# Hybrid decoder trunk on one core: the accumulating transfer of weight quarters one group earlier, and the hooks moved

## The chip, the cores and the metric

One core of one Trainium2 chip. The metric is the device time of one execution of the kernel in microseconds (us); a smaller number is better. Several executions are timed, and one more is recorded by the hardware profiler.

## The reference

Two layers on an activation of 512 tokens by 2048 features, all in float32. Each layer does one input projection, three parallel branches, and one output projection onto the residual stream:

```
h = _rmsnorm(x, norm_g)
proj = h @ w_in                      # 2048 x 7696
y_conv = B * conv3(C * h_conv) * silu(gate)          # 512 wide
y_sb   = stick_breaking(rms(q), rms(k), v) * silu(gate)   # 8 heads of 128, 128-query blocks
y_gla  = rms(gated linear attention(q, k, v, decay)) * silu(gate)   # 4 heads, chunks of 64
return x + concat(y_conv, y_sb, y_gla) @ w_out       # 2048 x 2048
```

## The kernel before

**Groups.** The columns of both weights are cut into groups of 256: 30 of `w_in` and 8 of `w_out` in a layer, taken in one fixed order in the list `specs`: the linear attention's groups and the first half of the convolution's, then v, g, q, k for each pair of heads (j = 0 to 3), the second half of the convolution, and the output groups gi = 0 to 7. Between the groups of one j and the next lies the attention of that pair of heads: query and key tiles are normalised (squares on ACT in L1318, scaling on DVE in L1332), cast (L1336 on ACT, L1337 on DVE), transposed by DMA from SP's queue (L1341) and multiplied into scores on TensorE (L1226).

**Precision by splits.** Float32 is kept by splitting each weight into an fp16 high part (ACT) and an fp16 rest (DVE). A normal group has one high and one rest for each half of its rows (L435, L442) and takes three matmul passes. The common scale of a group comes first: the sum of squares of both halves of its staged tile (`squares`: two ACT instructions, L366, 1.9 us each), a reduction over partitions on POOL (L380), and a few tiny steps on DVE (`wscale`, L383 to L398).

**Quick groups.** Some groups are multiplied by seven products instead of eight (`project_quick`): the 2 by 2 blocks b11, b12, b21, b22 of the group's weights are combined, and seven combinations are split (`split` in `wsums`: L485 on ACT, L486 on DVE, once each for parts 0 to 6, the last into `w7h` and `w7l`). They are g and k for each j and `conv h 1` in `w_in`, and gi = 3, 4, 6 in layer 0 and 3, 4, 5, 6 in layer 1 of `w_out`. In the input groups b12 + b11 is formed by a DMA that accumulates, L503 on POOL's queue (half a megabyte); in the output groups by DVE adds (L492 to L498). The products go into four accumulators: pa holds product 1, is copied to y12 by ACT (L778) and later copied to y11 (L785); pb, pd and pf follow.

**Order.** Loads (`fetch`, L355, two halves of 1 MB, issued from POOL) go two groups ahead into two staging buffers `st`. A quick group alters its staged tile in place and holds the buffer until its last split. Within a group, matmuls call `hook`, which pops functions from a list that `weights` fills: the first takes the squares of the next group, the second its scale and its splits. `order` ties an instruction behind the matmul of the hook. Each engine runs its own list in order, and POOL's list holds loads, reductions and the accumulating transfers together.

```
# weights(), before
if i + 2 < len(specs):
    with tc.high_priority():
        fetch(i + 2)
if i and i + 1 < len(specs):
    hooks.extend([lambda mm: squares(i + 1, mm), lambda mm: parts_of(i + 1, mm)])
```

Of the kernel before, what the change touches and what calls it, by code (L numbers as in the profile page):

```python
# [11 lines left out]
ALU = mybir.AluOpType  # L12
# [31 lines left out]
def hybrid_trunk(ctx, tc, x, norm_g, w_in, conv_w, conv_b, sb_qn_g, sb_kn_g,  # L44
# [145 lines left out]
    def order(a, b):  # L190
        tc.add_manual_dep(a.ins, b.ins.name, mybir.DependencyInfo(
            mybir.DependencyClass.NoSync, mybir.DependencyReason.DATA), reason="order")
# [254 lines left out]
    def squares(i, mm):  # L447

        with tc.high_priority():
            for h in range(2):  # L450
                a = wmax(i, h)
                if not h:
                    order(a, mm)
# [12 lines left out]
    def hook(mm):  # L466

        if hooks:
            hooks.pop(0)(mm)

    def wsums(i):

        sc = scales[i]
        b11, b12, b21, b22 = (whole[i][:, r::2, c * P:(c + 1) * P] for r in range(2) for c in range(2))
        parts = loaded[i][0]
        for _ in range(3):
            a = [wpool.tile([P, HK, GX], F16, tag=t, name=nm(t)).rearrange("p k c -> p (k c)") for t in ("wh", "wl")]
            parts.extend([p_[:, n * HK * P:(n + 1) * HK * P] for p_ in a] for n in range(2))
        parts.append([wk([P, HK * P], t, 1, dt=F16) for t in ("w7h", "w7l")])
        for n in range(7):  # L480
            parts[n] = [a.rearrange("p (k c) -> p k c", c=P) for a in parts[n]]

        def split(b, n):
            h_, l_ = parts[n]
            hi = S.activation(h_, b, AF.Copy, scale=sc)  # L485
            V.scalar_tensor_tensor(l_, b, sc, h_, ALU.mult, ALU.subtract)  # L486
            return hi


        if specs[i][1] is w_out:  # L490
            split(b11, 0)
            V.tensor_tensor(b11, b11, b12, ALU.add)  # L492
            split(b22, 3)
            V.tensor_tensor(b12, b12, b22, ALU.add)
            V.tensor_tensor(b22, b11, b22, ALU.add)
            split(b22, 1)
            split(b12, 2)
            V.tensor_tensor(b22, b22, b21, ALU.add)  # L498
            split(b21, 4)
            split(b11, 5)  # L500
            split(b22, 6)
            return
        G.dma_start(out=b12, in_=b11, accum_op=ALU.add)  # L503
        split(b11, 0)
        split(b22, 3)
        V.tensor_tensor(b22, b12, b22, ALU.add)  # L506
        split(b22, 1)
        V.tensor_tensor(b11, b22, b11, ALU.subtract)
        split(b11, 2)
        split(b21, 4)  # L510
        V.tensor_tensor(b21, b22, b21, ALU.add)
        split(b12, 5)
        split(b21, 6)

    def weights():

        i = cursor[0]
        cursor[0] += 1
# [3 lines that stand above are left out]
        assert not hooks  # L522
        if i and i + 1 < len(specs):
            hooks.extend([lambda mm: squares(i + 1, mm), lambda mm: parts_of(i + 1, mm)])
        return loaded.pop(i)

    fetch(0)
# [129 lines left out]
    for l in range(depth):  # L657
# [3 lines left out]
        def project_cols():  # L661

            w, u = weights()
            ps = [bank(psp, "p") for _ in range(2)]
            for h in range(2):
                wh, wl = w[h]
                for c, o in enumerate(ps):
                    cs = slice(c * P, (c + 1) * P)
                    for kk in range(HK):
                        k = h * HK + kk  # L670
                        st_ = (h == 0 and kk == 0)
                        en = (h == 1 and kk == HK - 1)
                        T.matmul(o, wh[:, kk, cs], xh[:, :, k, :], start=st_, stop=False)  # L673
                        T.matmul(o, wh[:, kk, cs], xl[:, :, k, :], start=False, stop=False)  # L674
                        mm = T.matmul(o, wl[:, kk, cs], xh[:, :, k, :], start=False, stop=en)  # L675
                        if not h and not c and kk in (0, HK - 1):
                            hook(mm)
            return ps, u

# [7 lines left out]
        def project_toks(ah, al, late=()):  # L687

            w, u = weights()
            ps = [bank(psp, "p") for _ in range(2)]  # L690
            rounds = [[k for k in range(h * HK, (h + 1) * HK) if k not in late] for h in range(2)] + [list(late)]
            lastk = [q for q in rounds if q][-1][-1]
            for ks in rounds:
                for t in range(NT):
                    o = ps[t // 2][:, (t % 2) * GW:(t % 2 + 1) * GW]
                    for k in ks:
                        mm = tok_mm(o, ah, al, w, t, k, GW, k == 0 and t % 2 == 0, k == lastk)
                        if not t and k == 0 or t == 1 and k == rounds[0][-1]:
                            hook(mm)
            return ps, u  # L700

# [47 lines left out]
        def project_quick(src, sums, y, cols):  # L749

            (w11, wT2, wT3, w22, w21, wt1, wT4), u = weights()
            (pa, pd), (pb, pf) = ([bk[:, n * GW:(n + 1) * GW] for n in range(2)]
                                  for bk in [bank(psp, "p") for _ in range(2)])
            a11, a12, a22 = ([a[:, 2 * r:2 * r + 2, c::2, :] for a in src] for r, c in ((0, 0), (0, 1), (1, 1)))
            s_, a21_22, a12_s, a11_21 = sums

            def prod(o, w, a, start, stop=False):
                for t in range(1 if cols else 2):
                    for kk in range(HK):
                        for i, (p_, q_) in enumerate(((0, 0), (0, 1), (1, 0))):  # L760
                            st_ = start and t == kk == i == 0
                            en = stop and kk == HK - 1 and i == 2
                            if cols:
                                mm = T.matmul(o, w[q_][:, kk, :], a[p_][:, :, kk, :], start=st_, stop=en,  # L764
                                              skip_group_check=True)
                            else:
                                mm = T.matmul(o[:, t * P:(t + 1) * P], a[p_][:, t, kk, :], w[q_][:, kk, :], start=st_,  # L767
                                              stop=en, skip_group_check=True)
                            if start and t == kk == 0 and i == 2 and o is pa:
                                hook(mm)  # L770
                return mm

            y11, y12, y21, y22 = (
                y[:, c, r * GW:(r + 1) * GW] if cols else y[:, 2 * r:2 * r + 2, c * P:(c + 1) * P]
                for r in range(2) for c in range(2))
            za, zb, zd, zf = (a if cols else a.rearrange("p (t c) -> p t c", c=P) for a in (pa, pb, pd, pf))
            prod(pa, w11, a11, True)
            S.activation(y12, za, AF.Copy)  # L778
            hook(prod(pb, wT2, s_, True))
            V.tensor_tensor(y21, zb, y12, ALU.subtract)  # L780
            prod(pd, wT3, a11_21, False)
            S.activation(y22, zd, AF.Copy)
            prod(pf, w22, a12_s, False)
            prod(pa, w21, a12, False)
            S.activation(y11, za, AF.Copy)  # L785
            prod(pb, wt1, a21_22, False, True)
            V.tensor_tensor(y12, zb, y12, ALU.subtract)
            V.tensor_tensor(y22, y12, y22, ALU.subtract)
            V.tensor_tensor(y12, zf, y12, ALU.add)
            yield 0, u  # L790
            prod(pd, wT4, a22, False, True)
            V.tensor_tensor(y21, zd, y21, ALU.subtract)
            yield 2, u
# [12 lines left out]
        def project_by_token(ah, al, n):  # L806

            w, u = weights()
            ps = []
            for t in range(NT):  # L810
                o = bank(psp, "p")
                for i, (a_, part) in enumerate(((ah, 0), (al, 0), (ah, 1))):
                    for k in range(KT):
                        mm = T.matmul(o[:, :n], a_[:, t, k, :], w[k // HK][part][:, k % HK, :n],  # L814
                                      start=i == 0 and k == 0, stop=i == 2 and k == KT - 1)
                        if not t and (not i and not k or i == 2 and k == KT - 1):
                            hook(mm)
                ps.append(o)
                yield t, o, u
# [611 lines left out]
```

## Time and profile before

| | |
|---|---|
| median of 3 runs | 1715.83 us (1713.79 to 1720.53) |
| the profiled execution | 1717.69 us |
| its span, first to last instruction | 1715.9 us |
| TensorE (PE) busy | 1669.9 us, 97% |
| VectorE (DVE) busy | 1331.3 us, 78% |
| ScalarE (ACT) busy | 1129.1 us, 66% |
| GpSimd (POOL) busy | 239.2 us, 14% |
| mean granted TensorE clock | 0.992 |

Busy times are shares of the span. In the lists of instructions a line reads: start, duration, engine, line of the kernel, operation, output<-input, and in brackets how long the engine was idle before it and what released it. A line of the waits reads: engine, tile and line, what it waited for, then us in total, times, longest. "DMA to landing" is the time from a transfer's issue to its landing, shortest, median and longest of the selection.

### The profile page before, as it was taken

To read this page: it belongs to the slowest core of one execution; us is meant where nothing else is said; L and a number is where in the kernel's file an instruction comes from. 1 tells how busy PE (TensorE), PEld (TensorE's weight loads), DVE (VectorE), ACT (ScalarE), POOL (GpSimd) and SP (SyncE) were. 2 spreads that over 40 slices of the span, in tenths; PEclk is the share of its full clock that TensorE was granted. 3 is DMA by queue.
4 is the path that set the end of the run, shared out by engine and by line. 5 is a ranking of instruction groups with operands and counts; after the bars stand their busy time and mean duration, and the time that the engine had idled before them with its cause. 6 is when DMAs were issued, how large, how long until landed. Compare 5 with 4: busy or idle time off the path is not lost.

```text
span 1715.9 us, 36876 instructions
## 1 busy us (share of the span) xinstructions
PE 1669.9 (97%) x15642; PEld 1298.4 (76%) x15642; DVE 1331.3 (78%) x2327; ACT 1129.1 (66%) x1619; POOL 239.2 (14%) x286
## 2 busy tenths in 40 slices
PE   7999999999999989999989999999999999899999
PEld 5644548989898964799976455689898889548998
DVE  8975889877878767785688677997786888677883
ACT  7667677767666656666665676776765767565662
POOL 1211111111111111001122101121111111101110
PEclk9999999999999999999999999999999999999999
DMA  7233323566766686245543332446666667753441
GB/s 251 83 114 98 99 64 99 145 116 152 136 149 139 147 233 164 77 150 181 186 103 108 116 102 75 118 123 125 148 136 105 146 132 150 201 153 108 162 151 50
DMA packets 181478, 227.26 MB, mean 132 GB/s; under 512 B 94194, under 2 KB 141628, under 8 KB 180800
## 3 DMA queue, kind: packets, MB, share of 16 engines
q0 software_dynamic: 60352, 168.83, 34.4%
q1 hardware_dynamic: 111952, 46.61, 14.4%
q10 hardware_dynamic: 9008, 9.45, 1.7%
q8 instruction: 122, 2.00, 0.5%
q14 instruction: 44, 0.36, 0.1%
HBM read 179.65 MB, written 14.68 MB: 113 GB/s over the span
## 4 chain that ended last, share of the span: by engine, by line
PE 73%; DVE 12%; DMA 7%; ACT 4%; issue 3%; POOL 0%; DVEq 0%; ACTq 0%
PE psp L767 13%; PE psp L674 8%; PE psp L675 8%; PE psp L673 8%; PE psp L685 7%; PE psp L684 7%; PE psp L683 7%; PE psp L814 6%; PE psp L764 3%; DMA st<-in_w_in_dram 2%; DVE wl L486 2%; DMA th<-za 2%; DMA kT<-qp 2%; ACT junk L366 1%; DVE wl L442 1%
## 5 line engine op out<-in xcount | busy, mean ns | idle before, releaser
L366 ACT ACTIVATE junk<-st 128x2048 uint8<-128x2048 f32 x150 | 285.1, 1901 | 44.1 <-DMA st<-in_w_in_dram 42.8
L442 DVE SCALAR_TENSOR_TENSOR wl<-st,ws,wh 128x2048 f16<-128x2048 f32 x102 | 239.2, 2347 | 80.7 <-ACT wh L435 80.7
L435 ACT ACTIVATE wh<-st,ws 128x2048 f16<-128x2048 f32 x100 | 199.3, 1998 | 105.4 <-PE psp L674 47.1
L684 PE MATMUL psp<-wl,m 128*128 128x256 f16 x960 | 261.7, 273 | 0.0
L683 PE MATMUL psp<-wh,m 128*128 128x256 f16 x960 | 261.7, 273 | 0.0
L685 PE MATMUL psp<-wh,m 128*128 128x256 f16 x960 | 261.7, 273 | 0.0
L485 ACT ACTIVATE wh<-st,ws 128x1024 f16<-128x1024 f32 x150 | 167.6, 1143 | 120.5 <-DVE st L506 57.7
L486 DVE SCALAR_TENSOR_TENSOR wl<-st,ws,wh 128x1024 f16<-128x1024 f32 x150 | 189.6, 1279 | 27.4 <-ACT wh L485 27.3
L355 POOL DMA_DIRECT2D st<-in_w_in_dram x114 | 102.2, 900 | 436.0 <-DVE wl L442 319.4
L683 PE MATMUL psp<-wh,x 128*128 128x256 f16 x512 | 139.6, 273 | 0.0
L684 PE MATMUL psp<-wl,x 128*128 128x256 f16 x512 | 139.6, 273 | 0.0
L685 PE MATMUL psp<-wh,x 128*128 128x256 f16 x512 | 139.6, 273 | 0.0
L675 PE MATMUL psp<-x,wl 128*128 128x512 f16 x352 | 134.4, 382 | 2.2 <-DVE zun L186 2.2
L674 PE MATMUL psp<-x,wh 128*128 128x512 f16 x352 | 134.4, 382 | 0.0
L673 PE MATMUL psp<-x,wh 128*128 128x512 f16 x352 | 134.0, 381 | 0.0
L673 PE MATMUL psp<-m,wh 128*128 128x512 f16 x352 | 133.9, 380 | 0.0
L674 PE MATMUL psp<-m,wh 128*128 128x512 f16 x352 | 133.9, 380 | 0.0
L675 PE MATMUL psp<-m,wl 128*128 128x512 f16 x352 | 133.9, 380 | 0.0
L675 PEld LDWEIGHTS <-wl 128*128 128x128 f16 x704 | 69.2, 98 | 85.0 <-DVE wl L442 2.7
L673 PEld LDWEIGHTS <-wh 128*128 128x128 f16 x704 | 69.2, 98 | 81.5 <-issue 3.1
L380 POOL PARTITION_ALL_REDUCE wgm<-wm x75 | 40.0, 533 | 648.2 <-ACT junk L366 633.6
L674 PEld LDWEIGHTS <-wh 128*128 128x128 f16 x704 | 69.2, 98 | 80.8 <-issue 2.3
(427 smaller groups left out, 4042.2 us busy)
## 6 DMA issues: line engine op xcount, KB each, us to landing
st<-in_w_in_dram POOLq DMA_DIRECT2D x114, 1024.0 KB, 8.4
st<-in_w_out_dram POOLq DMA_DIRECT2D x32, 1024.0 KB, 7.4
st<-st POOLq DMA_DIRECT2D x18, 512.0 KB, 8.3
st<-in_w_in_dram SPq DMA_DIRECT2D x6, 1024.0 KB, 12.0
mixd<-g POOLq DMA_DIRECT2D x24, 256.0 KB, 7.7
x<-in_x_dram SPq DMA_DIRECT2D x4, 1024.0 KB, 4.9
qT<-in_x_dram ACTq DMA_DIRECT2D x8, 512.0 KB, 3.8
qT<-xs ACTq DMA_DIRECT2D x8, 512.0 KB, 3.9
```

Source lines behind the costliest of these rows:

```text
L366: sq = S.activation(junk(HK * GW).rearrange("p (k n) -> p k n", k=HK), staged[i][h], AF.Square, accum_out=peak[i][:, h:h + 1])
L435: hi = S.activation(wh[:, :, :GW], staged[i][h], AF.Copy, scale=scales[i])
L442: V.scalar_tensor_tensor(wl[:, :, :GW], staged[i][h], scales[i], wh[:, :, :GW], ALU.mult, ALU.subtract)
L485: hi = S.activation(h_, b, AF.Copy, scale=sc)
L486: V.scalar_tensor_tensor(l_, b, sc, h_, ALU.mult, ALU.subtract)
L673: T.matmul(o, wh[:, kk, cs], xh[:, :, k, :], start=st_, stop=False)
L674: T.matmul(o, wh[:, kk, cs], xl[:, :, k, :], start=False, stop=False)
L675: mm = T.matmul(o, wl[:, kk, cs], xh[:, :, k, :], start=False, stop=en)
L683: T.matmul(o, ah[:, t, k, :], wh[:, kk, :n], start=st_, stop=False, skip_group_check=True)
L684: T.matmul(o, ah[:, t, k, :], wl[:, kk, :n], start=False, stop=False, skip_group_check=True)
L685: return T.matmul(o, al[:, t, k, :], wh[:, kk, :n], start=False, stop=en, skip_group_check=True)
L767: mm = T.matmul(o[:, t * P:(t + 1) * P], a[p_][:, t, kk, :], w[q_][:, kk, :], start=st_, stop=en, skip_group_check=True)
```

## The change

The transfer that adds b11 into b12 becomes a function of its own, `fold`, and a third hook. `weights` appends it for the group after next, so it is issued one group ahead of its scale, before the squares of its group, which therefore are taken over a tile whose b12 already holds the sum. The output groups use the same transfer and the same order of splits as the input groups; the DVE adds that were theirs alone go (four adds become three). In `project_quick` the first hook (squares of the next group) moves behind the copy of product 1 to y12, the second (scale and splits) behind product 3, the third (the new one) behind product 5. The three normal projections get a third place where `hook` is called.

```diff
+    def fold(i, mm):
+        b11, b12 = (whole[i][:, ::2, c * P:(c + 1) * P] for c in range(2))
+        order(G.dma_start(out=b12, in_=b11, accum_op=ALU.add), mm)
...
-        if specs[i][1] is w_out:
-            split(b11, 0)
-            V.tensor_tensor(b11, b11, b12, ALU.add)
-            split(b22, 3)
-            V.tensor_tensor(b12, b12, b22, ALU.add)
-            V.tensor_tensor(b22, b11, b22, ALU.add)
-            split(b22, 1)
-            split(b12, 2)
-            V.tensor_tensor(b22, b22, b21, ALU.add)
-            split(b21, 4)
-            split(b11, 5)
-            split(b22, 6)
-            return
-        G.dma_start(out=b12, in_=b11, accum_op=ALU.add)
         split(b11, 0)
         split(b22, 3)
         V.tensor_tensor(b22, b12, b22, ALU.add)
         split(b22, 1)
         V.tensor_tensor(b11, b22, b11, ALU.subtract)
         split(b11, 2)
         split(b21, 4)
         V.tensor_tensor(b21, b22, b21, ALU.add)
         split(b12, 5)
         split(b21, 6)
...
             hooks.extend([lambda mm: squares(i + 1, mm), lambda mm: parts_of(i + 1, mm)])
+        if i + 2 in quick:
+            hooks.append(lambda mm: fold(i + 2, mm))
...   # project_cols
-                        if not h and not c and kk in (0, HK - 1):
+                        if not c and kk in ((HK - 1,) if h else (0, HK - 1)):
...   # project_toks
-                        if not t and k == 0 or t == 1 and k == rounds[0][-1]:
+                        if not t and k == 0 or t == 1 and k in (rounds[0][-1], rounds[1][-1]):
...   # project_quick
-                            if start and t == kk == 0 and i == 2 and o is pa:
-                                hook(mm)
...
             prod(pa, w11, a11, True)
-            S.activation(y12, za, AF.Copy)
-            hook(prod(pb, wT2, s_, True))
+            hook(S.activation(y12, za, AF.Copy))
+            prod(pb, wT2, s_, True)
             V.tensor_tensor(y21, zb, y12, ALU.subtract)
-            prod(pd, wT3, a11_21, False)
+            hook(prod(pd, wT3, a11_21, False))
             S.activation(y22, zd, AF.Copy)
             prod(pf, w22, a12_s, False)
-            prod(pa, w21, a12, False)
+            hook(prod(pa, w21, a12, False))
...   # project_by_token
-                        if not t and (not i and not k or i == 2 and k == KT - 1):
+                        if not t and not i and not k or t < 2 and i == 2 and k == KT - 1:
```

## The prediction

> **What bounds the kernel now.** I read the page first, then TensorE's waits, then the ordered lists of ACT, DVE, POOL and SP around one attention step, and last the output projection's end. The page:
>
> ```profile
> PE 1669.9 (97%) x15642; PEld 1298.4 (76%) x15642; DVE 1331.3 (78%) x2327; ACT 1129.1 (66%) x1619; POOL 239.2 (14%) x286
> ...
> L366 ACT ACTIVATE junk<-st 128x2048 uint8<-128x2048 f32 x150 | 285.1, 1901 | 44.1 <-DMA st<-in_w_in_dram 42.8
> ...
> L486 DVE SCALAR_TENSOR_TENSOR wl<-st,ws,wh 128x1024 f16<-128x1024 f32 x150 | 189.6, 1279 | 27.4 <-ACT wh L485 27.3
> ...
> st<-in_w_in_dram POOLq DMA_DIRECT2D x114, 1024.0 KB, 8.4
> ```
>
> TensorE is busy 97%; all its idle time is 1715.9 - 1669.9 = 46 us. The matmuls stay the same in number, so the change can only move idle time and what idle time does to the clock. TensorE's waits, with what released each (total, times, longest), and two more from the list of all waits:
>
> ```profile
> PE psz L1226 <- DMA kT<-qp: 11.0, 2, 5.9
> PE psp L764 <- ACT g L785: 5.5, 6, 1.9
> ...
> PE psm L1263 <- DVE e L1270: 3.6, 1, 3.6
> ...
> PE psp L767 <- DVE wl L486: 1.3, 1, 1.3
> ```
> ```profile
> ACT junk L366 <- DMA st<-in_w_in_dram: 42.8, 17, 5.6
> ...
> DVE st L506 <- DMA st<-st: 0.3, 1, 0.3
> ```
>
> and, from the view of line L503 alone, how long its 18 transfers took from issue to landing:
>
> ```profile
> DMA to landing us min/median/max: 6.7/8.3/14.7
> ```
>
> Two readings. ACT stands 42.8 us in the squares L366, waiting for weights to land; behind it stands the copy L785 that frees a PSUM bank, and TensorE loses 5.5 us to that. The accumulating transfer L503, on the other hand, is hidden today: DVE waits 0.3 us for it.
>
> **Squares out of the way of PSUM copies: a gain.** In the changed order, squares stand behind the first PSUM copy of a quick group, or behind the attention work, no longer ahead of L785. I count all 5.5 us as gained (0 if ACT stands elsewhere instead). The 1.3 us of L767 came from a part that was late in layer 0's output projection; the earlier fold saves one DVE add there, so I count it as gone too. Together -6.8. Seven adds leave the output groups' DVE work, 7 x 1.22 us by the L506 row below, but DVE is at 78% and no wait of TensorE on those adds is listed: worth nothing by themselves.
>
> **Squares now wait for the fold.** This is the cost. One attention step (layer 0, j=1, gate group g): POOL, then SP, ACT and DVE (start, duration, engine, line), then the transfers' landings, the g load first, the fold second:
>
> ```profile
> 422.32 1.82 POOL L355 DMA_DIRECT2D st<-in_w_in_dram  x2 [3.23 <-DVE qrm L211]
> ...
> 438.74 0.40 POOL L380 PARTITION_ALL_REDUCE wgm<-wm  x1 [5.73 <-ACT junk L366]
> 439.52 1.60 POOL L503 DMA_DIRECT2D st<-st  x1 [0.38 <-issue]
> ...
> 467.74 1.80 POOL L355 DMA_DIRECT2D st<-in_w_in_dram  x2 [7.62 <-DVE w7l L486]
> ```
> ```profile
> 443.92 4.77 SPq L1341 DMA_TRANSPOSE kT<-qp  x2
> ```
> ```profile
> 433.23 1.89 ACT L366 ACTIVATE junk<-st 128x2048 uint8<-128x2048 f32 x1
> ...
> 436.29 0.29 ACT L1318 ACTIVATE e<-kT 128x128 f32<-128x128 f32 x1
> ...
> 436.58 1.89 ACT L366 ACTIVATE junk<-st 128x2048 uint8<-128x2048 f32 x1
> ...
> 440.42 1.15 ACT L485 ACTIVATE wh<-st,ws 128x1024 f16<-128x1024 f32 x1 [1.24 <-DVE ws L396]
> ...
> 442.84 1.06 ACT L1336 ACTIVATE qp<-kT 128x1024 f16<-128x1024 f32 x1 [1.27 <-DVE kT L1332]
> ```
> ```profile
> 440.62 2.19 DVE L1332 SCALAR_TENSOR_TENSOR kT<-kT,qr,kg 128x128 f32<-128x128 f32 x8
> ...
> 446.67 1.23 DVE L506 TENSOR_TENSOR st<-st 128x1024 f32<-128x1024 f32 x1 [0.32 <-DMA st<-st]
> ```
> ```profile
> DMA to landing us min/median/max: 6.0/7.6/9.3
> ```
> ```profile
> DMA to landing us min/median/max: 7.1/7.1/7.1
> ```
>
> The load's second half was issued at 423.2 and landed 9.3 us later, at 432.5; the squares began at once. In the changed build the fold is POOL's next step after that landing: 432.6 + 7.1 = 439.7, and the first squares cannot start before it, 6.5 us later than now. Queued behind them on ACT, in the built order: six of the eight kT squares (L1318), the second half's squares, the g activation, splits, and the kT cast L1336. On DVE, the scale of g stands ahead of L1332. So: 439.7 + 1.9 + 6 x 0.29 + 1.9 = 445.3 for the end of the squares, where it was 438.5. From there L1336 came 4.4 us later (442.84): now 449.7. SP's transposes began 1.1 us behind it: 450.8. TensorE needs their result here (first row: the scores' span; then the duration of one transpose, min/median/max; then how long one took to land at 443.92, and another one, at 1204.6 in layer 1):
>
> ```profile
> L1226 PE MATMUL psz<-kT,qT x24: 219/300/379, 454.1 to 462.5; 128*128 128x512 f16 x6, 128*128 128x384 f16 x6, 128*128 128x128 f16 x6, 128*128 128x256 f16 x6
> ```
> ```profile
> L1341 SPq DMA_TRANSPOSE kT<-qp x16: 1232/1868/8405, 357.8 to 1489.0; - x16
> ```
> ```profile
> DMA to landing us min/median/max: 7.9/7.9/7.9
> ```
> ```profile
> DMA to landing us min/median/max: 3.3/3.3/3.3
> ```
>
> The second transpose goes 1.23 us after the first, at 452.0, and lands at 455.3 with the short landing: 1.2 us behind 454.1. With the 7.9 us behind the first issue it is 458.7, 4.6 us late. I take the short one, 1.3 us, because the fold has landed before the transposes start, whereas now (439.5 to 446.6) it runs into them. Six g groups go this way (j=0 to 2 of both layers): +8, bounds 0 and 28, not counting the clock.
>
> **The k groups.** There no kT work is queued behind the squares, but the weights themselves come later. Behind the fold now stand only the add L506 and part 1's split: 1.2 + 1.15 + 1.28 = 3.7 us. Changed: squares 3.8, all-reduce and scale 1.4 to 1.7 (from 438.74 to the split at 440.42, with other work between), splits of parts 0 and 3 (2.4 + 1.3), add 1.2, part 1 2.4: about 13 us. The k group of j=1 was loaded at 467.74, second half 0.9 later; with 8.4 us to land (the page's median for such loads) and 8.3 for the fold, 485.3; part 1 is ready at 498.3. The second product reads it from 501.4 on:
>
> ```profile
> L767 PE MATMUL psp<-wh,s x128: 219/219/219, 501.4 to 516.3; 128*128 128x128 f16 x128
> ```
>
> Three us of slack. In layer 1 a fold (issued at 1326.0) landed late, and it was behind the 3.6 us of L1263 above, DVE standing in L506 meanwhile:
>
> ```profile
> DMA to landing us min/median/max: 14.7/14.7/14.7
> ```
>
> That wait leaves DVE's queue, but with 13 us behind such a landing in place of 3.7 the three us of slack are more than gone: 9.3 - 3, some 6 us late. So -3.6 + 6.3, taken as +3; bounds -3.6 (no fold lands late) and +10 (two do).
>
> **The output projection, layer 1.** Four quick groups (gi 3 to 6) follow each other. The 1344 matmuls took this long in all, so a group is 18.9 us and a product 2.7:
>
> ```profile
> 1600.00:1716.00 116.00, 75.65 (x1344) 75.24 (x1344) 1.00 0.37 122
> ```
> ```profile
> 1621.99 1.78 POOL L355 DMA_DIRECT2D st<-in_w_out_dram  x2 [2.18 <-DVE wl L486]
> ...
> 1641.56 1.78 POOL L355 DMA_DIRECT2D st<-in_w_out_dram  x2 [2.08 <-DVE wq L392]
> ```
> ```profile
> 1653.79 1.89 ACT L366 ACTIVATE junk<-st 128x2048 uint8<-128x2048 f32 x1
> ...
> 1657.72 1.13 ACT L485 ACTIVATE w7h<-st,ws 128x1024 f16<-128x1024 f32 x1
> 1658.76 0.36 ACT L778 ACTIVATE g<-psp 128x256 f32<-128x256 f32 x1
> ```
> ```profile
> 1632.73 0.42 DVE L788 TENSOR_TENSOR g<-g 128x256 f32<-128x256 f32 x1
> ```
> ```profile
> DMA to landing us min/median/max: 6.2/8.0/9.7
> ```
>
> (the last row is the load at 1641.56).
>
> Quick group gi=3 starts at 1616.0 (1691.6 less four groups). A staging buffer comes free with part 7's split, which in the new order stands between the two squares of the next group; and the all-reduce of those squares stands ahead of the next load on POOL. So the chain is load, fold, squares, load. First product and copy end at 1619.1; squares 1.9, part 7's halves 1.1 + 1.3: the load of gi=5 starts at 1623.6 (1622.0 now). Its second half lands 10 us later, 1633.7; fold 7.7, between 7.1 and the median of 8.3: 1641.4. Squares, part 7, squares, all-reduce: 5.4; the load of gi=6 starts at 1646.8 (1641.56 now). It lands 0.9 + 9.7 later, 1657.4; fold 7.1: 1664.5. First squares then, 10.7 us after the 1653.8 of now. Squares, part 7, squares, all-reduce, scale: 1.9 + 1.1 + 1.9 + 0.5 + 0.9, 1670.8. Part 0: 1.15 + 1.28, 1673.2; part 3, 1674.5. The built order for gi=6 then puts three adds (3.7), parts 4 and 5 (2.6) and four combining steps of 0.42 (1.7) ahead of part 1 (1.3): 1683.8. TensorE's second product wants part 1 at 1616.0 + 3 x 18.9 + 2.7 = 1675.4, 1676.6 with 1.2 of delay before it. A stall of 7.2 us; bounds 2 (fold and loads at their shortest) and 11. So long a stall costs clock as well. After the 3.6 us stall of L1263 the granted clock (third number from the end) was
>
> ```profile
> 1354.00:1358.00 4.00, 3.78 (x33) 3.49 (x34) 1.75 (x7) 4.00 (x13) 0.39 (x1) 0.66 0.01 4
> ```
>
> that is 4 x 0.34 = 1.4 us lost, and some in the next stretch: add 1.7. The three other folded output groups that can be late (gi=4 of both layers, gi=6 of layer 0) do not stand at the end of two such links, since a normal group's load or work lies between, and lose only through the new order of parts: 0 to 2.6 us (two splits of 1.28), I take 1.2 each, 3.6. Together +12.5.
>
> **Sum.** -6.8 + 8 + 3 + 12.5 = +16.7 us. The profiled execution took 1717.7 us (span 1715.9 and 1.8 around it), 1.9 above the median of the runs, 1715.8. Against the median: 1732.5; I say 1732. Own range 1721 to 1743. A measurement of this kernel tells about 0.5%, 8.6 us, from no change: 1707.2 to 1724.4.
>
> **What the Trainium skill says against this.** The folds above took 6.7 us at the shortest and 8.3 at the median, for 512 KB. The Trainium skill, "DMA: Bandwidth & Descriptors", section "Anatomy of one DMA", fits such a transfer at 2.0 us + bytes / 436e3 per us; for 512 KB that is an estimate of 3.2 us. By it every fold would land about 4 to 5 us earlier than in my working, and nearly all of the stalls would go, leaving some 1709. The trace so far does not bear it out: no L503 landed in under 6.7 us.
>
> **Rivals.**
> *The fold is fast when it runs alone (0.17).* Moved ahead, it no longer collides with transposes and mixd stores. If it lands some 4 us sooner than 7.1, the g and k delays fall below the slack, and gi=6 is just in time. Then the gains stand alone: 6.8, the 3.6 of L1263 and its 1.7 of clock: -12.1 from the median, some 1703.7. For it: the transposes at 443.92 were under way with the fold of 439.52; against it: the shortest of 18 is 6.7. It decides where the squares' delay at g, 6.5 us, falls under 5.3, what the short landing of the transposes leaves.
> *It cancels (0.21).* The gains of 6.8 stand, the g steps lose nothing (transposes land in time), the k groups nothing, gi=6 stalls 5 and the order of parts costs 2: +0.2, so 1716. For it: 1.2 us of lateness at g is less than the spread of the loads' landings (9.1 to 9.7 in two of the rows). Against it: each term of the working has to fall on its low side.
> *Much slower (0.16).* The transposes land late as at 443.92: 4.6 us in each g step, over what dropped the clock at L1263, so 6.3. Half of the six at that price make 19 - 4 = +15 more, 1747; all six 1762. Decided where the transposes take over 5.6 us from their issue. I put it at 1748.
> *My case* has 0.46.
>
> **How the numbers follow.** The range 1706 to 1749 leaves out about half of the first and third rival, 0.16, and little of the rest. Faster by over 0.5%: 0.14 of the first rival and 0.02 of the second, 0.16. Slower: all of the third, 0.39 of mine, 0.02 of the second, 0.57. The rest, 0.27, is the same.
>
> **What would show it.** In the changed profile the waits of L366 on a load should turn into waits on the fold (st<-st), and L764's wait on the y11 copy should vanish. The scores should wait for the kT transposes in the g steps, about a microsecond each; TensorE should stop in the second product of the last quick output group for 5 to 9 us. I am wrong if the fold lands in under 5 us, if the squares never wait for it, or if TensorE's idle total falls below 40 us.

## The result, and the profile after

The changed kernel takes 1771.2 us at the median (1765.0 to 1777.0, 4 runs) where the kernel before takes 1715.2: 1.032 times as long, 95% interval 1.028 to 1.036. The forecast was 1732 us, range 1706 to 1749. The profiled execution has a span of 1767.6 us, 51.7 more than before.

The page of the changed kernel, engines and the squares' group:

```profile
PE 1684.0 (95%) x15642; PEld 1306.1 (74%) x15642; DVE 1324.1 (75%) x2320; ACT 1128.2 (64%) x1619; POOL 248.8 (14%) x293
...
L366 ACT ACTIVATE junk<-st 128x2048 uint8<-128x2048 f32 x150 | 285.8, 1905 | 98.5 <-DMA st<-st 81.0
```

The number of matmuls is the same, but TensorE is idle for 1767.6 - 1684.0 = 84 us, where it was idle for 46. Its busy time rose by 14 us too, with as many matmuls. Each matmul is recorded longer (219 ns) than the distance to the next (56 ns in a running product), so that the records can take short stops for work; that this is all of the 14 us is an inference, and the clock, 0.991 where it was 0.992, explains some 2 of them at most. The squares now stand 81 us in front of the fold. The view of the fold's own line says who waited for it and how long it took to land:

```profile
  ACT junk L366: 81.0, 16
```
```profile
DMA to landing us min/median/max: 6.4/7.7/11.6
```

TensorE's waits in the changed kernel (L760 are the products of a quick group over tokens, L769 and L776 the copies to y12 and y11, L491 the splits' rests, L1217 the scores):

```profile
PE psz L1217 <- DMA kT<-qp: 12.1, 12, 2.1
PE psp L760 <- DVE wl L491: 12.0, 12, 2.8
PE psp L760 <- ACT kT L776: 7.1, 8, 1.3
PE psp L760 <- ACT kT L769: 6.8, 5, 1.4
PE psp L760 <- ACT raw L1305: 6.5, 2, 3.8
```

The old wait of L764 on y11, 5.5 us, is gone, as was to be expected. In its place stand five kinds of short waits, four of them inside the quick groups over tokens. Those that name kT or raw are in k groups, those on raw in the two groups of j=0; of the 12.0 us on L491, 7.5 are in k groups and 4.5 in the output groups.

To see where the 51.7 us arose, both traces are divided at landmarks: the first matmul of product 1 and the last of product 7 of each quick group. Differences from the kernel before, us:

| stretch | forecast | changed |
|---|---|---|
| eight k groups, first to last product | +3 | +36.7 |
| from a k group to the next g group (v and the scores), six | +8 | +9.5 |
| g groups and the q groups behind them, eight | -5.5 | -1.9 |
| quick output groups of both layers | +11.2 (12.5 less 1.3) | +11.2 |
| conv h 1 and what stands before it | 0 | +3.9 |
| from conv h 1 to the output projection | 0 | -9.4 |
| the rest | 0 | +1.6 |

One term is out by an order of magnitude. The others are near their forecasts, or offset each other in part. In the k groups TensorE's recorded idle time rose from 3.6 to 31.7 us; by the granted clock of the eight stretches, some 5 us more went to a lower clock (an estimate: 6.8 us lost, before 1.7).

**One k group, before and after.** Layer 0, j=1. ACT before: the splits of parts 0 and 3, and the copy to y12.

```profile
400.40 2.19 ACT L485 ACTIVATE wh<-st,ws 128x1024 f16<-128x1024 f32 x2 [0.51 <-DVE ws L396]
...
418.43 0.36 ACT L778 ACTIVATE kT<-psp 128x256 f32<-128x256 f32 x1
```

The group began on TensorE at 412.7, so the splits began 12.3 us ahead of it, and the copy came 5.7 us after its start. In the changed kernel the group begins at 424.2. POOL, ACT and last TensorE:

```profile
394.03 1.79 POOL L355 DMA_DIRECT2D st<-in_w_in_dram  x2 [1.56 <-DVE wq L392]
401.30 1.76 POOL L355 DMA_DIRECT2D st<-in_w_in_dram  x2 [5.48 <-DVE g L778]
404.21 1.57 POOL L474 DMA_DIRECT2D st<-st  x1 [1.15 <-DMA st<-in_w_in_dram]
```
```profile
415.55 1.91 ACT L366 ACTIVATE junk<-st 128x2048 uint8<-128x2048 f32 x1 [3.36 <-DMA st<-st]
...
420.77 2.19 ACT L490 ACTIVATE wh<-st,ws 128x1024 f16<-128x1024 f32 x2 [1.18 <-DVE ws L396]
...
427.07 3.21 ACT L490 ACTIVATE wh<-st,ws 128x1024 f16<-128x1024 f32 x3
...
431.99 0.36 ACT L769 ACTIVATE kT<-psp 128x256 f32<-128x256 f32 x1
```
```profile
432.39 0.22 PE L760 MATMUL psp<-wh,s 128*128 128x128 f16 x1 [1.36 <-ACT kT L769]
```

The fold was issued at 404.2, landed at 415.5, and the splits began 3.4 us ahead of the group, 9 us later than they used to. Everything on ACT behind them is late with them, the copy to y12 too. Product 1 had ended near 427; its copy came at 432.0, 7.8 us after the start of the group, and TensorE stopped for it.

### The profile page after: what moved, and what is told of

Its sections match the earlier page's. It is cut to its first block, busy times and chain, and to the rows that moved or that the text cites. A ratio compares the mean times of both kernels' runs of the same rounds, so it can differ in the third digit from the quotient of the medians.

```text
span 1767.6 us, 36866 instructions
## 1 busy us (share of the span) xinstructions
PE 1684.0 (95%) x15642; PEld 1306.1 (74%) x15642; DVE 1324.1 (75%) x2320; ACT 1128.2 (64%) x1619; POOL 248.8 (14%) x293
## 5 line engine op out<-in xcount | busy, mean ns | idle before, releaser
L366 ACT ACTIVATE junk<-st 128x2048 uint8<-128x2048 f32 x150 | 285.8, 1905 | 98.5 <-DMA st<-st 81.0
L491 DVE SCALAR_TENSOR_TENSOR wl<-st,ws,wh 128x1024 f16<-128x1024 f32 x150 | 188.9, 1280 | 19.4 <-ACT wh L490 19.1
L355 POOL DMA_DIRECT2D st<-in_w_in_dram x114 | 106.4, 973 | 483.9 <-DVE wl L442 258.8
L760 PEld LDWEIGHTS <-s 128*128 128x128 f16 x1536 | 92.8, 101 | 27.1 <-issue 27.0
```

The costliest lines, as they stand in the source:

```text
L366: sq = S.activation(junk(HK * GW).rearrange("p (k n) -> p k n", k=HK), staged[i][h], AF.Square, accum_out=peak[i][:, h:h + 1])
```

## The experiments

Two theories. A: the squares' wait for the fold makes the scale of a group late, and with it ACT's whole list; most of that in the k groups. B: the moved hooks put squares and splits of the next group in front of PSUM copies. The edits:

```diff
# squares free of the fold (first run), over the rows of b21 and b22
-        sq = S.activation(junk(HK * GW)..., staged[i][h], AF.Square, ...)
+        src = staged[i][h][:, 1::2, :] if i in quick else staged[i][h]
+        kk = HK // 2 if i in quick else HK
+        sq = S.activation(junk(kk * GW)..., src, AF.Square, ...)
```

> The changed kernel, but the squares of a quick group are taken over the rows of b21 and b22 alone, which the fold does not touch, so they never wait for it (b11 and b12 are left out of the sum of squares, and each of those squares takes about 1.0 us in place of 1.9). Everything else stays: early fold, moved hooks, output groups folded by DMA. Theory A (the wait of the squares for the fold is the cost, about 37 us of it in the eight k groups): 1705 to 1722 us, the waits of L366 on st<-st gone, k groups back to 20 us each. Theory B (the moved hooks are the cost, since squares and splits of the next group now stand ahead of PSUM copies on ACT): 1750 to 1771 us.

1693.8 us, 0.987 of the kernel before (0.983 to 0.990): faster than both kernels. This is what theory A says, and the gain is larger than it expected.

The hooks alone, in the kernel before (`hook(S.activation(y12, ...))` and the later places, fold and output groups as they were):

> The kernel before with the hooks alone moved as in the change; the fold stays behind the scale and the output groups keep their DVE adds. Theory A: 1708 to 1722 us (the 5.5 us of the y11 copy may be gained). Theory B: 1750 us or more.

1726.9 us, 1.005 (1.003 to 1.007). Neither theory had this: not B's 50 us, but not A's gain either. The y11 waits went, the k groups were 2.7 us shorter, and the stretch of conv h 1 lost 10.3 us. Its splits, behind the later hook, began 6.3 and 7.0 us ahead of the group (layers 0 and 1), where they had begun 11.5 and 11.3 ahead; its fold took 13 us, was 6.7, and landed 4 to 5 us after the group had begun. TensorE's largest wait in that run, all of it in conv h 1:

```profile
PE psp L764 <- ACT wh L485: 15.3, 4, 4.6
```

The other half, the fold early and the hooks put back:

```diff
-            hook(S.activation(y12, za, AF.Copy))
-            prod(pb, wT2, s_, True)
+            S.activation(y12, za, AF.Copy)
+            hook(prod(pb, wT2, s_, True))
...
# and the first hook back at the first matmuls of product 1
```

> The changed kernel with the two hooks of squares and splits in project_quick put back to where they were before; the fold stays one group ahead and the squares wait for it. Theory A: 1755 to 1780 us. Theory B: 1710 to 1725 us.

1794.3 us, 1.044 (1.041 to 1.047). This speaks clearly against B, and it is worse than A said. A reading, not tried alone: with squares asked for earlier, an ACT blocked on the fold holds up more. Its squares waited 75 us for the fold (81 in the changed kernel); TensorE's longest waits were

```profile
PE psz L1219 <- ACT zw L1229: 15.9, 6, 3.3
PE psm L1256 <- DVE e L1263: 14.8, 6, 2.8
```

that is, attention work. TensorE's idle time rose to 98.5 us from 84, and the granted clock fell to 0.976 from 0.991, so the difference is not waits alone. With the early fold, the moved hooks kept the change from costing 23 us more.

The k groups alone put back (`if i + 2 in quick - kgroups` for the early fold, the fold of k behind its scale):

> The changed kernel, but the k groups keep the fold where it was before, behind their scale; g, conv h 1 and the output groups are folded early. Theory A with its place in the k groups: 37 us less than the changed kernel at most and 28 at least, 1734 to 1743 us. If the cost is spread over all folded groups alike (8 of 25 are k): 16 us less, 1755. Theory B: no change, 1765 to 1775.

1731.4 us, 40 us less than the changed kernel, a little more than the 28 to 37 expected. By landmarks the k groups fell from +36.7 to +3.7.

Were the shorter squares the gain of the first run? The same, each of the squares taken twice:

```diff
+        if i in quick:
+            for r in range(2):
+                a = S.activation(junk(...), staged[i][h][:, 1::2, :], AF.Square, accum_out=peak[i][:, h:h + 1])
+            return ...
```

> The changed kernel with the squares of a quick group over the rows of b21 and b22 alone, as in the run without the wait, but each of them taken twice, so that ACT works as long as in the changed kernel (2 x 1.0 against 1.9 us). b11 and b12 are left out of the sum of squares. If the wait for the fold is what costs, nearly all of the 77 us between the changed kernel and that run stay gained: 1694 to 1712 us. If the shorter squares did it, the time is back near 1771, at least 1745.

1700.5 us, 0.989 (0.985 to 0.994). ACT's busy time in it is 1144.2 us, 16 more than in the changed kernel, and yet it is 71 us faster: it is the wait that costs. Its k group of j=1 began at 413.3, with

```profile
400.16 2.35 ACT L496 ACTIVATE wh<-st,ws 128x1024 f16<-128x1024 f32 x2 [0.26 <-DVE ws L402]
...
416.17 0.39 ACT L775 ACTIVATE kT<-psp 128x256 f32<-128x256 f32 x1
```

splits 13.1 us ahead, and the copy the moment product 1 had ended. And the short squares in the kernel before:

> The kernel before with the squares of the quick groups over the rows of b21 and b22 alone (b11 and b12 left out of the sum; 25 groups x 2 x 0.9 us = 45 us less ACT work, and nothing else). If shorter squares are worth something by themselves, what is gained here is that part of the 23 us by which the run without the wait beat the kernel before: 1706 to 1716 us by the theory that the wait and the early fold do it; 1694 if it is all ACT time.

1723.7 us, 1.003 (1.001 to 1.005). ACT's busy time is 1091.6 us, 37.5 less than in the kernel before, and it gains nothing. Neither expectation had it a little slower: the stretch of the g and q groups grew by 7.6 us, for a cause that stays open.

The squares moved ahead of the fold, one group early:

```diff
...   # the first hook then takes no squares for such a group
-            hooks.append(lambda mm: fold(i + 2, mm))
+            hooks.append(lambda mm: (squares(i + 2, mm), fold(i + 2, mm)))
```

> The changed kernel, but the squares of a quick group are taken one group ahead too, over the loaded tile and ahead of its fold, by the third hook; nothing is left out of the sum. The squares wait for the load alone, the fold for the squares. Theory A (the wait of the squares for the fold): 1695 to 1715 us, the waits of L366 on st<-st gone. If an ACT queue blocked on any late tile costs as much, 1735 or more.

1730.0 us, 1.007 (1.005 to 1.009), between the two expectations. The waits on the fold are gone, but ACT now blocks on loads, in the group ahead, and PSUM copies stand behind it:

```profile
ACT junk L366 <- DMA st<-in_w_in_dram: 47.4, 22, 4.9
```
```profile
PE psp L763 <- ACT kT L779: 9.5, 6, 1.9
...
PE psp L760 <- ACT g L779: 7.0, 7, 2.4
```

Is the fold late in the k groups because the next load goes ahead of it? That load put behind it (`order(d, folded[i - 1])`):

> The changed kernel with the load of the group behind a k group put behind that k group's fold on POOL's queue; in the changed kernel the load goes first and the fold landed 10.6 to 11.6 us after its issue. If that collision makes the k groups' folds late, they land 7 to 8 us after issue here and about 3 us are gained in each of eight: 1742 to 1755 us. If the fold's landing is not what delays k, 1765 to 1778.

1765.3 us. The collision went,

```profile
DMA to landing us min/median/max: 6.4/7.5/7.9
```

but the time fell by 6 us where 16 to 29 were expected if the collision mattered, and by landmarks the k groups lost 36.0 us as against 36.7. The second branch held: the collision is not the main cost. The folds of j=1 to 3 landed 1.0 to 4.3 us earlier against their groups, and their splits began 0 to 3.2 us earlier. With that, TensorE no longer waits for a part in these groups, so product 2 has its weights in time. It stops at the copy of product 1 instead (L776 is the copy to y12 here):

```profile
PE psp L767 <- ACT kT L776: 15.1, 6, 2.6
```

These are 2.3 to 2.6 us in each of the six groups of j=1 to 3, where the changed kernel had 6.8 us in five. The copy still comes 7.4 to 9.7 us after the start of the group (7.6 to 8.9 in the changed kernel).

Which groups? Squares free of the fold in the k groups alone, then in the g groups alone:

> The changed kernel with the squares of the eight k groups alone taken over the rows of b21 and b22, twice, so that they do not wait for the fold and cost as much (b11 and b12 of these groups are left out of the sum); all other folded groups wait as in the changed kernel. If the k groups carry the loss, as the times between landmarks of the two traces say (37 of 52 us): 1728 to 1742 us. If g carries it through the kT transposes, which is what was forecast: 1765 to 1771.

> The same for the eight g groups alone. By the landmarks (9.5 us in the stretches of v and the scores): 1757 to 1765 us. If g carries most of the loss: 1735 or less.

1729.6 and 1746.1 us. With k free its stretch goes from +36.7 to -2.7, and the scores still wait, as in the changed kernel:

```profile
PE psz L1226 <- DMA kT<-qp: 12.2, 14, 2.5
```

With g free that wait falls from 12.1 us to 3.6, all of it behind conv h 1, the stretch of v and the scores goes from +9.5 to -0.9, and k stays at +33.0. The gain by the median, 25 us, is above the 6 to 14 expected. The profiled execution took 1753.2 us, the longest of the four, and where the rest of the gain arose stays open.

The old hooks with free squares:

> Early fold, squares over the rows of b21 and b22 alone, once (b11 and b12 left out of the sum), with the two hooks of project_quick where they were before. Beside the run with the same squares and the moved hooks (1694 us) it prices the hooks: moved alone they cost 10 us. If that cost is theirs in any company: 1684 to 1690 us. If it came only from the late folds of conv h 1, which the early fold removes, the moved hooks gain their 5 us at the y11 copy: 1697 to 1705 us.

1709.0 us, 0.996 (0.994 to 0.998), against 1693.8 with the moved hooks. So the moved hooks gain 15 us once the fold is early and no squares wait for it, and cost 10 us where the fold is late. The second reading had the direction; the gain is larger than the 5 us it gave.

What was still open was whether late squares are enough. In the kernel with free squares of full cost, those of the k groups were taken four and six times, so that their scale is late through ACT work, with no transfer in the way:

> The kernel in which no squares wait for the fold (squares over the rows of b21 and b22, taken twice, b11 and b12 left out of the sum, 1700 us), with the squares of the eight k groups taken four times in place of two: their scale comes about 4.4 us later by ACT work alone. If lateness of the scale is what costs: with the slack of some 6 us before product 3 needs the y12 copy, 0 to 10 us more, 1700 to 1710. If the cost came from something else about the transfer: 1700.

> The same with six takes: the scale of the k groups about 8.8 us later, as late as it is in the changed kernel (420.6 there, 12 us of shift taken off, against 400 here). If lateness alone costs: 25 to 40 us more than 1700, 1725 to 1740. If not: 1700 to 1710.

1704.3 and 1744.9 us. The second one's scale (DVE) and the copy to y12 (ACT), for the group that begins at 413.4:

```profile
409.18 0.15 DVE L405 TENSOR_SCALAR ws<-wq 128x1 int32<-128x1 int32 x1
```
```profile
420.15 0.36 ACT L778 ACTIVATE kT<-psp 128x256 f32<-128x256 f32 x1
```

Here the splits begin 4.0 us ahead of the group, close to the 3.4 of the changed kernel, the copy comes 6.7 us after its start, and the group took 24.6 us (25.1 there; 20.7 with free squares). The k groups lost 32 us in all against the run with free squares, 4.0 each on the mean, and 7 us at the smaller delay, 0.9 each. (Some 20 of the 44 us by which this run is slower arose elsewhere, behind conv h 1, in waits of the scores on kT.) So squares that end late on ACT cost time with no transfer in the way. The run makes both the scale and ACT's list late and does not part the two.

It does not reproduce the whole loss, though. Lost against the run with free squares, in us:

| k groups | changed kernel | six takes |
|---|---|---|
| j=1 and 2, four groups | 18.3 | 15.7 |
| j=3, two groups | 8.5 | 14.3 |
| j=0, two groups | 15.6 | 2.2 |

In j=1 and 2 the loss is the same in kind and nearly in size. In j=3 each group of the six takes has a stop of 3.3 us of the attention's values on DVE (L1263) that the changed kernel does not have there. In j=0 late squares alone cost about 1 us a group, although the splits begin 5.8 us ahead of the group, as late as in the changed kernel (5.9 and 4.8). What is different there in the changed kernel is what stands behind the squares. ACT in layer 0, and TensorE:

```profile
315.82 1.91 ACT L366 ACTIVATE junk<-st 128x2048 uint8<-128x2048 f32 x1 [8.45 <-DMA st<-st]
...
322.87 1.34 ACT L827 ACTIVATE ga<-g,wu 128x512 f32<-128x512 f32 x2
...
333.87 1.15 ACT L490 ACTIVATE wh<-st,ws 128x1024 f16<-128x1024 f32 x1 [2.71 <-DVE st L497]
334.93 0.58 ACT L1305 ACTIVATE raw<-psp 128x512 f32<-128x512 f32 x1
```
```profile
335.56 0.22 PE L760 MATMUL psp<-wh,s 128*128 128x128 f16 x1 [2.74 <-ACT raw L1305]
```

The activation of the gate (L827) stands behind the blocked squares, and DVE's work for the gate and the linear attention follows it; the add L497 comes behind that work, part 1 behind the add, and behind part 1 the copy of q (L1305) that frees a PSUM bank. With six takes the gate's activation runs between the takes, 14.6 us ahead of the group; in the changed kernel it starts 7.1 us ahead. That the wait for the fold is what costs in j=0 too, the run with k free shows: both groups take 19.3 us there, 26.6 and 27.7 in the changed kernel. The chain behind it is read from the trace and not tried.

**A version that takes every weight into the scale.** Squares over b11 and the rows of b21 and b22, which need no fold, and for b12 its largest magnitude squared, by DVE, ahead of the fold:

```diff
-        order(G.dma_start(out=b12, in_=b11, accum_op=ALU.add), mm)
+        bmax[i] = sm(1, "wb", 2)
+        order(V.tensor_reduce(bmax[i], b12, AX.XY, ALU.max, apply_absolute_value=True), mm)
+        V.tensor_tensor(bmax[i], bmax[i], bmax[i], ALU.mult)
+        G.dma_start(out=b12, in_=b11, accum_op=ALU.add)
...
# and in wscale: the all-reduced bmax is added to the sum of squares
```

> The changed kernel, with the squares over b11 and over the rows of b21 and b22, and in place of the squares of b12 its largest magnitude squared, taken by DVE ahead of the fold and added into the scale: nothing of the weights is left unbounded, and ACT never waits for the fold. It pays 25 DVE reductions of about 1.2 us, which wait for the load, and a second all-reduce on POOL. If a wait of DVE for the load is cheap: 1695 to 1712 us. If DVE blocked on the load costs as ACT blocked on the fold did: 1735 or more.

1707.5 us, 0.994 (0.990 to 0.997): a little faster than the kernel before, and 64 us faster than the changed one. DVE waits 29.8 us for loads of `w_in` in the new reduction and TensorE shows no wait on it:

```profile
DVE wb L484 <- DMA st<-in_w_in_dram: 29.8, 12, 3.9
```

## Why the prediction was wrong

The direction was right, and so was the first half of the mechanism: the squares wait for the fold, and that is the cost. What that wait holds up in the k groups was wrong, and with it the size, 56 us of loss where 17 were forecast.

**The k groups (+3, bounds -3.6 and +10; measured +36.7).** This step failed. Its 13 us from the fold's landing to part 1 was right: 415.5 to about 428.2 in the group above. Its "three us of slack" was not, for two reasons.

The smaller one is the landing. The group that the prediction worked out, which it calls that of j=1, is that of j=2: its second product starts at 501.4, and the k group of j=1 begins at 412.7. The prediction has its fold landed 13.4 us ahead of the group; in the changed kernel it landed 8.6 ahead, after 10.6 us where 8.3 were taken, with the next load ahead of it on POOL. But the run without that collision shows that this is the smaller part: product 2 had its part in time in j=1 to 3, and the k groups lost as much.

The larger one is that slack was counted to part 1 and product 2 alone. What TensorE needs next, the copy of product 1 to y12, stands on ACT behind all the splits but the last, and behind the squares of q's norm. The squares behind the fold made this whole list some nine us late, and TensorE paid at several points of the same group: by the waits on record, 7.5 us for late parts, 6.8 and 7.1 for the copies to y12 and y11, 6.5 for the copy of q. The run with six takes shows that late squares do this by themselves in j=1 and 2. In j=0, where 16.5 of the 36.7 us arose, the gate's work stood behind the squares too; "no kT work is queued behind the squares" is true there, but other work is. The gain of 3.6 us at L1263 came about: no such stop is left in the k groups.

**The g groups (+8; measured +9.5).** The step held, its choice of the short landing too. In the attention step of j=1, layer 0, ACT stood 8.9 us for the fold, and the transposes landed quickly:

```profile
456.01 1.91 ACT L366 ACTIVATE junk<-st 128x2048 uint8<-128x2048 f32 x1 [8.85 <-DMA st<-st]
```
```profile
DMA to landing us min/median/max: 3.3/3.3/3.3
```

There the scores waited 0.8 us for them (1.2 forecast). The run with g free confirms the cause.

**The output projection (+12.5 less 1.3; measured +11.2).** Right in sum, in part by luck. The chain load, fold, squares, load is there. But gi=6 of layer 1 grew by 5.0 us, 3.2 of stops and an estimate of 1.7 of clock, where 7.2 and 1.7 were forecast; gi=5 grew by 2.0 where nothing was forecast, for a copy to y22 that stood behind squares waiting for the fold, and gi=4 by 2.3 where 1.2 were. The folds landed in 6.4 to 6.5 us, not 7.1 to 7.7, and the load of gi=6 went out at 1688.3, 30.0 us behind the start of gi=3, as worked out (1646.8 less 1616.0 is 30.8). The last stop came on part 1, as forecast:

```profile
1725.55 0.22 PE L760 MATMUL psp<-wl,zw 128*128 128x128 f16 x1 [2.78 <-DVE wl L491]
```

**The gain at the PSUM copies (-5.5; measured -1.9).** The waits on y11 left the g groups, but k groups have them now (L776, 7.1 us). The whole gain in this stretch shows in runs with moved hooks in which no squares wait for the fold: -6.9 with free squares, -7.4 with the hooks alone.

**Not seen: -9.4 behind conv h 1.** Two long waits of the scores on kT (11.0 us in the kernel before) fall to short ones. No run was made for it alone.

**The rivals.** The fast fold fell: no fold in the changed kernel took under 6.4 us. The fit in the Trainium skill, "DMA: Bandwidth & Descriptors", "Anatomy of one DMA", gives an estimate of 3.2 us for this size and does not hold for this transfer, which accumulates. "It cancels" fell with the sum. The much slower case, 1747 to 1762, was passed, but not by its mechanism: the transposes landed early, and the stops that made it were in the k groups. None of the three signs of being wrong came: no fold under 5 us, squares that do wait, 84 us of idle time. They test the wait and not its price.

## What to carry to other kernels

Before an operation is made to wait for a transfer, follow what stands behind it on its engine to the last thing that another engine needs, not to the first: slack is that of the tightest consumer in the list, and a list that runs nine us late can be paid for at several of its consumers. A transfer that is hidden stays hidden only as long as what reads its result stands late; starting it earlier is worth something if its readers stay where they were, and here the squares could be kept off it. Two edits that are judged together can have opposite signs: the moved hooks cost 10 us alone and gained 15 with the early fold and squares that do not wait for it.

## What the runs showed of the hardware

The same accumulating transfer of 512 KB took 6.4 to 8.2 us outside the k groups and 10.1 to 11.6 in six of the eight k groups, where a load of 2 MB had just been issued; with that load put behind it, none took over 7.9. That was not in the forecast. TensorE's recorded busy time rose from 1669.9 to 1684.0 us with the same matmuls and nearly the same mean clock (0.992 and 0.991); that the 14 us are short stops that the records do not show as idle is an inference. And after the stop of 2.7 us in the k group of j=0, layer 0, matmuls ran at a granted clock of 0.51 (the third number from the end; the row has the length of the stretch, then the busy times of PE, PEld, DVE, ACT and POOL) some two us later:

```profile
337.60:341.00 3.40, 3.27 (x34) 3.11 (x32) 2.48 (x3) 3.40 (x7) 0.00 (x0) 0.51 0.00 0
```
